# Eight swiglu blocks of a layer as seven-product pairs instead of seven, three plain blocks instead of four, one block instead of three left for the end

## The chip, the cores and the metric

The kernel runs on one core of a Trainium2 chip. The metric is the device time of one execution in microseconds (us); the kernel before was timed three times.

## The reference, cut to what matters

Two layers, each `x += mixer(rmsnorm(x))` and then `x += swiglu(rmsnorm(x))`, on x of 256 frames by 2048 features in float32. The change lies in the second half of both layers:

```
def swiglu(h, w1, w3, w2):
    return (jax.nn.silu(h @ w1) * (h @ w3)) @ w2
```

h is 256 x 2048, w1 and w3 are 2048 x 5632, w2 is 5632 x 2048. The 5632 columns are worked in eleven blocks of 512, numbered 0 to 10.

## The kernel before, in words

**A product.** Every float32 weight tile (128 x 2048, 1 MB) is loaded by a DMA on SP's queue and split into two fp32r parts: ScalarE casts it (`wh`), VectorE subtracts to get the rest (`wl`), both in `split_w` (line 132). Each product then runs three matmuls (high by high, high by low, low by high). A ring of four `raw` tiles holds streamed weights, and rings of three hold `wh` and `wl`.

**Two ways to make a block of w1 and w3.** With the frames cut into two halves and the 2048 inputs into two halves, h @ w1 and h @ w3 of a block are eight half products of 24 matmuls. A plain block does all eight, 192 matmuls and eight splits. `pair` (line 368) does the two weights together with seven products, 168 matmuls, from sums of weights: it splits 14 tiles, forms four sums on VectorE (`plus`, line 405) and four by DMAs on GpSimd's queue that add to what lies in SBUF (`plus_dma`, line 408). Its products run in the order A11, F5, F3, A12, F6, F7, N22. A11 is followed by the sums va + vb, F3 by vb + vc. A DMA adds to va after F5, for F6, and another after F6, for N22. After A12 to N22 come the gates (`done`), which make the block's values. va and vb lie in four tiles of their own (`v0` to `v2`, and `g3`), vc and vd in the raw ring.

**Turning.** A finished block's values are transposed on TensorE and split again (`split_t`, line 208; `turned` in `plain_steps`, line 515), as the left operand of the down product by w2. These steps wait in the queue `side`; `tick`, called after every six or twelve matmuls, runs the next one.

**Order of a layer's swiglu** (`ffn`, line 561). First block 0 by `plain` (line 451), alone. Its first two tiles run before the norm of x is complete (`flush`, then `rstd`). Then seven turns, each a pair with other work between its products: the pair yields after every product, and the work does one step of 24 matmuls in each of eight slots. The work is either a plain block in eight steps (`plain_steps`, line 480) or eight pieces of the down product (`pieces`, line 535), which takes two turned blocks at a time and adds to x:

```
enumerate(((2, 1), (3, None), (4, None), (6, 5), (7, None), (8, None), (10, 9)))
```

The first number is the pair's block, the second the plain block beside it (None: pieces). A pair yields twice after F7, so a turn runs A11, step 0, F5, 1, F3, 2, A12, 3, F6, 4, F7, 5, 6, N22, 7. The three blocks left (8, 9, 10) go to `residual` (line 345), which multiplies them by w2 with nothing beside it. In the first layer this also makes the next norm's operands; in the second it ends with `gemm_tail` (line 140), which does the first 128 frames, then the others, and `last` (line 1125), which scales and stores the result.

The order of instructions on each engine is not quite the program's: at compile time a scheduler lets a later instruction pass an earlier one that it thinks is not ready.

Of the kernel before, what the change touches and what calls it, by code (L numbers as in the profile page):

```python
# [19 lines left out]
P = 128  # L20
# [3 lines left out]
NB = 512  # L24
# [31 lines left out]
def trunk(  # L56
# [55 lines left out]


    side = deque()

    def tick():

# [14 lines left out]
    def split_w(raw, pool=wp):  # L132

        wh = pool.tile([P, 4, NB], F32R, tag="wh", bufs=3 if pool is wp else 1, name="wh")
        wl = pool.tile([P, 4, NB], F32R, tag="wl", bufs=3 if pool is wp else 1, name="wl")
        nc.scalar.copy(wh, raw)  # L136
        nc.vector.tensor_sub(wl, raw, wh.bitcast(F32))  # L137
        return wh, wl

    def gemm_tail(w, c0, parts, pool, done):  # L140
# [228 lines left out]
    def pair(nrm, wa, wb, c0, turn, done):  # L369
# [33 lines left out]
            return nrm.pool.tile([P, NB], F32, tag=tag, bufs=1, name=tag)  # L403

        def plus(dst, other):
            return lambda c: nc.vector.tensor_add(dst[c], dst[c], other[c])  # L406

        def plus_dma(dst, w, j):
            return lambda c: nc.gpsimd.dma_start(dst[c], src(w, j, c), accum_op=ALU.add)
# [30 lines left out]
        product(b3, vb, "F7", False, True)  # L440
        nc.vector.tensor_add(y, y, b3)
        yield
        yield
        product(b3, va, "N22", False, True)
        nc.vector.tensor_sub(s1, s1, b3)
        done("21", s1)
        done("22", y)
        yield

    def plain(nrm, ws, c0, done):  # L450

        for q, w in zip("12", ws):
            acc = [acc_p.tile([P, NB], F32, tag="acc", name="acc") for _ in range(3)]
            for g in range(4):
                raw = wp.tile([P, 4, NB], F32, tag="raw", bufs=RAW, name="raw")
                nc.sync.dma_start(raw, w[g * NB:(g + 1) * NB, c0:c0 + NB].rearrange("(k p) n -> p k n", p=P))
                wh, wl = split_w(raw)
                for bank, form, start, stop in ((0, "A11", True, True), (1, "F7", True, True)) if g < 2 else \
                        ((0, "A12", False, True), (2, "N22", True, True)):
                    hi, lo = nrm.forms[form]  # L460
                    for j in range(4):
                        k = 4 * (g % 2) + j
                        for i, (l_, r_) in enumerate(((hi, wh), (hi, wl), (lo, wh))):
                            nc.tensor.matmul(acc[bank], l_[:, k, :], r_[:, j, :], start=start and k == i == 0,  # L464
                                             stop=stop and k == 7 and i == 2, skip_group_check=not start)
                        if j % 2:
                            tick()
                if g == 1:
                    s1 = nrm.pool.tile([P, NB], F32, tag="s1", bufs=1, name="s1")
                    nc.scalar.copy(s1, acc[0])  # L470
                    nc.vector.tensor_add(s1, s1, acc[1])
                    yield
            nc.vector.tensor_sub(s1, s1, acc[2])
            done("1" + q, acc[0])
            done("2" + q, s1)

    def plain_steps(ws, b, forms, sc, ready):

        flat = res.tile([P, 4 * NB], F32, tag=f"g{b % 3}", name="early")
        us = [flat[:, t * NB:(t + 1) * NB] for t in range(NT)]  # L480
# [51 lines left out]
            yield  # L532

        part = [None, None, b * NB]
        side.append(turned())
        yield part

    def pieces(w, parts):

# [21 lines left out]
    def ffn(layer, nrm):  # L561

        w1, w3, w2 = ffn_w1[layer], ffn_w3[layer], ffn_w2[layer]
        sc = {}
        parts = []
        ready = set()

        def block(b, us):
            def turned():
                yield from split_t(us, hi, lo)  # L570
                ready.add(b * NB)

            hi, lo = hi_lo(b % 3)
            side.append(turned())
            parts.append((hi, lo, b * NB))

        def gate(us):
            def done(q, v):
                t = int(q[0]) - 1
                if q[1] == "1":  # L580
                    us[t] = cm.tile([P, NB], F32, tag="u", name="u")
                    nc.scalar.activation(us[t], v, AF.Silu, scale=sc["r"][:, t:t + 1])
                else:
                    nc.vector.scalar_tensor_tensor(us[t], us[t], sc["r"][:, t:t + 1], v, op0=ALU.mult, op1=ALU.mult)
            return done

        us = [None] * NT
        for slot, _ in enumerate(plain(nrm, (w1, w3), 0, gate(us))):
            if slot == 0:
                flush()  # L590
                sc["r"] = nrm.rstd()
        block(0, us)

        for turn, (b, inner) in enumerate(((2, 1), (3, None), (4, None), (6, 5), (7, None), (8, None), (10, 9))):
            if inner is None:
                two, parts[:2] = parts[:2], []
                work = pieces(w2, two)
            else:
                work = plain_steps((w1, w3), inner, nrm.forms, sc, ready)
            us = [None] * NT  # L600
            made = None
            for slot, _ in enumerate(pair(nrm, w1, w3, b * NB, 1 - turn % 2, gate(us))):
                if inner is None and slot == 0:
                    assert all(r0 in ready for _, _, r0 in two)
                made = next(work)
            if inner is not None:
                parts.append(made)
            block(b, us)
        return w2, parts


# [554 lines left out]
```

## Time and profile before

| | us |
|---|---|
| median of 3 runs | 2260.61 (2259.99 to 2260.88) |
| the profiled execution | 2262.72 |
| its span | 2260.9 |
| TensorE busy | 2226.0 (98%), 10247 matmuls and transposes |
| VectorE busy | 1576.4 (70%) |
| ScalarE busy | 1169.4 (52%) |
| GpSimd busy | 100.1 (4%) |
| DMA | 484.96 MB, 214 GB/s on average |

The span runs from the first to the last instruction; the execution's own time has 1.8 us around it. The mean granted TensorE clock is 0.999 of full speed. A matmul shown as busy for 0.39 us overlaps the next one, so a busy share of 98% does not say by itself that TensorE is at its limit: the distance from the start of one to the start of the next does. In the rows below, PE is TensorE (PEld its weight loads), DVE VectorE, ACT ScalarE, POOL GpSimd, SP the engine that issues most loads.

### The profile page before, as it was taken

What the parts mean: (1) busy time and instruction counts of PE and PEld (TensorE: products, weight loads), DVE (VectorE), ACT (ScalarE), POOL (GpSimd) and SP (SyncE); (2) the same over time, 40 slices, a digit from 0 to 9 for tenths busy, and PEclk for the clock granted to TensorE, in tenths of its full rate; (3) what the DMA queues carried; (4) which work ended last, traced back from release to release, by engine and by line L of the source; (5) the groups of instructions that cost most, each with busy time, mean ns of one, the idle gap of its engine ahead of it and who ended that gap; (6) DMA issues with size and microseconds to landing.
All of it is one profiled execution on the core that took longest, in us unless ns stands there. A gap on an engine that the chain in (4) does not pass through costs nothing.

```text
span 2260.9 us, 25126 instructions
## 1 busy us (share of the span) xinstructions
PE 2226.0 (98%) x10247; PEld 1834.7 (81%) x10247; DVE 1576.4 (70%) x1282; ACT 1169.4 (52%) x1046; POOL 100.1 (4%) x147
## 2 busy tenths in 40 slices
PE   9999999999999999999999999999999999999998
PEld 8888888887787887788888888888888778778787
DVE  6546455778878888876555755556887886887874
ACT  5545455555555555555444544555554555555553
POOL 0000000000000000000100000000000000000000
PEclk9999999999999999999999999999999999999999
DMA  8555465597797797795554555457779779779763
GB/s 289 169 170 188 128 229 184 200 290 223 231 290 219 233 276 228 230 264 179 176 181 150 185 169 168 160 194 242 200 212 313 212 217 310 213 219 304 222 203 111
DMA packets 250547, 484.96 MB, mean 214 GB/s; under 512 B 8072, under 2 KB 20704, under 8 KB 250304
## 3 DMA queue, kind: packets, MB, share of 16 engines
q1 hardware_dynamic: 219856, 423.33, 54.3%
q0 software_dynamic: 29568, 58.72, 15.0%
q8 instruction: 80, 1.31, 0.2%
q10 hardware_dynamic: 1008, 1.31, 0.2%
q14 instruction: 35, 0.29, 0.0%
HBM read 481.20 MB, written 2.12 MB: 214 GB/s over the span
## 4 chain that ended last, share of the span: by engine, by line
PE 81%; DVE 11%; DMA 3%; ACT 2%; issue 2%; SPq 0%; POOL 0%; POOLq 0%; ACTq 0%
PE acc L394 15%; PE acc L202 12%; PE acc L204 12%; PE acc L203 12%; PE half L494 9%; DVE wl L137 4%; PE down L552 4%; PE down L553 4%; PE down L551 4%; DMA raw<-in_ffn_w 3%; PE acc L464 3%; DVE v L406 2%; ACT wh L136 2%; DVE g L406 1%; DVE x L558 1%
## 5 line engine op out<-in xcount | busy, mean ns | idle before, releaser
L136 ACT CAST wh<-raw 128x2048 fp32r<-128x2048 f32 x187 | 358.0, 1915 | 439.4 <-PE down L553 164.3
L137 DVE TENSOR_TENSOR wl<-raw,wh 128x2048 fp32r<-128x2048 f32 x187 | 426.8, 2289 | 204.1 <-ACT wh L136 203.9
L193 DVE TENSOR_TENSOR wl<-raw,wh 128x2048 fp32r<-128x2048 f32 (+3 forms) x161 | 349.9, 2176 | 302.2 <-ACT wh L192 302.1
L192 ACT CAST wh<-raw 128x2048 fp32r<-128x2048 f32 (+3 forms) x161 | 291.9, 1816 | 261.5 <-PE acc L204 211.0
L202 PE MATMUL acc<-wh,hh 128*128 128x512 f32 (+3 forms) x832 | 325.5, 391 | 0.0
L204 PE MATMUL acc<-wh,hl 128*128 128x512 f32 (+3 forms) x832 | 317.3, 381 | 0.0
L203 PE MATMUL acc<-wl,hh 128*128 128x512 f32 (+3 forms) x832 | 316.3, 380 | 0.6 <-DVE wl L193 0.6
L137 DVE TENSOR_TENSOR wl<-v,wh 128x2048 fp32r<-128x2048 f32 x102 | 232.8, 2287 | 24.5 <-ACT wh L136 24.4
L136 ACT CAST wh<-v 128x2048 fp32r<-128x2048 f32 x102 | 195.2, 1913 | 76.6 <-PE acc L394 43.4
L552 PE MATMUL down<-wl,g 128*128 128x512 f32 x512 | 201.3, 393 | 13.7 <-DVE wl L137 13.5
L553 PE MATMUL down<-wh,g 128*128 128x512 f32 x512 | 199.6, 390 | 0.0
L551 PE MATMUL down<-wh,g 128*128 128x512 f32 x512 | 198.3, 391 | 0.0
L203 PEld LDWEIGHTS acc<-wl,hh 128*128 128x128 f32 x832 | 156.7, 188 | 29.5 <-issue 1.7
L204 PEld LDWEIGHTS acc<-wh,hl 128*128 128x128 f32 x832 | 156.3, 188 | 29.5
L202 PEld LDWEIGHTS acc<-wh,hh 128*128 128x128 f32 x832 | 156.5, 188 | 28.6 <-issue 1.9
L394 PE MATMUL acc<-wh,fhF 128*128 128x512 f32 x448 | 174.6, 390 | 0.0
L394 PE MATMUL acc<-wl,fhF 128*128 128x512 f32 x448 | 174.3, 389 | 0.0
L394 PE MATMUL acc<-wh,flF 128*128 128x512 f32 x448 | 174.3, 389 | 0.0
L202 PE MATMUL acc<-wh,g 128*128 128x512 f32 x424 | 167.0, 394 | 0.0
L203 PE MATMUL acc<-wl,g 128*128 128x512 f32 x424 | 165.8, 391 | 0.0
L204 PE MATMUL acc<-wh,g 128*128 128x512 f32 x424 | 165.6, 391 | 0.0
L552 PEld LDWEIGHTS down<-wl,g 128*128 128x128 f32 x512 | 96.1, 188 | 39.2 <-DVE wl L137 20.2
(311 smaller groups left out, 3608.5 us busy)
## 6 DMA issues: line engine op xcount, KB each, us to landing
raw<-in_ffn_w SPq DMA_DIRECT2D x208, 1024.0 KB, 7.0
raw<-in_dsa_w_in SPq DMA_DIRECT2D x48, 1024.0 KB, 5.0
v<-in_ffn_w SPq DMA_DIRECT2D x42, 1024.0 KB, 8.4
raw<-in_gla_w_in SPq DMA_DIRECT2D x40, 1024.0 KB, 5.1
v<-in_ffn_w POOLq DMA_DIRECT2D x40, 1024.0 KB, 9.0
raw<-in_gla_w_out SPq DMA_DIRECT2D x16, 1024.0 KB, 5.0
g<-in_ffn_w POOLq DMA_DIRECT2D x16, 1024.0 KB, 13.0
raw<-in_dsa_w_out SPq DMA_DIRECT2D x16, 1024.0 KB, 4.9
```

The source lines that it names most:

```text
L136: nc.scalar.copy(wh, raw)
L137: nc.vector.tensor_sub(wl, raw, wh.bitcast(F32))
L192: a = nc.scalar.copy(wh[:, sl, :n], raw[:, sl, :n])
L193: v = nc.vector.tensor_sub(wl[:, sl, :n], raw[:, sl, :n], wh[:, sl, :n].bitcast(F32))
L202: nc.tensor.matmul(acc[t][:, :n], hi[:, k, ts_], wh[:, k, :n], start=start, stop=False)
L203: nc.tensor.matmul(acc[t][:, :n], hi[:, k, ts_], wl[:, k, :n], start=False, stop=False)
L204: nc.tensor.matmul(acc[t][:, :n], lo[:, k, ts_], wh[:, k, :n], start=False, stop=last)
L394: nc.tensor.matmul(acc, l_[:, k, :], r_[:, j, :], start=start and k == i == 0, stop=stop and k == 7 and i == 2, skip_group_check=not start)
L494: nc.tensor.matmul(acc[bank], l_[:, k, :], r_[:, j, :], start=start and k == i == 0, stop=stop and k == 7 and i == 2, skip_group_check=not ...
L551: nc.tensor.matmul(acc[t], hi[:, k, ts_], wh[:, k, :], start=start, stop=False)
L552: nc.tensor.matmul(acc[t], hi[:, k, ts_], wl[:, k, :], start=False, stop=False)
L553: nc.tensor.matmul(acc[t], lo[:, k, ts_], wh[:, k, :], start=False, stop=last)
```

## The change

Block 0 is no longer made alone. Its plain steps run beside the pair of block 1: two steps ahead of the pair, then one in six of its eight slots (not in slots 3 and 7). A layer is eight turns: pairs 1, 2, 4, 5, 6, 8, 9, 10; plain blocks 0, 3, 7 beside three of them, pieces beside the other five, so that ten blocks instead of eight are multiplied by w2 beside pairs and one, block 10, is left to `residual`. `plain` goes. The second yield after F7 moves behind N22: N22, step 6, step 7, and the next pair's A11. VectorE's sums are put into a queue, `sums_due`, and `split_w` issues one at the end of each later split, so a sum stands behind the next tile's split. A finished block's turning enters `side` after the next pair's A11 (slot 0), where it entered ahead of it. The DMA loads and the DMA additions of a pair are issued as before.

```diff
     side = deque()
+    sums_due = deque()
...
         nc.scalar.copy(wh, raw)
         nc.vector.tensor_sub(wl, raw, wh.bitcast(F32))
+        if sums_due:
+            sums_due.popleft()()
         return wh, wl
...
         def plus(dst, other):
-            return lambda c: nc.vector.tensor_add(dst[c], dst[c], other[c])
+            return lambda c: sums_due.append(lambda: nc.vector.tensor_add(dst[c], dst[c], other[c]))
...
         product(b3, vb, "F7", False, True)
         nc.vector.tensor_add(y, y, b3)
         yield
-        yield
         product(b3, va, "N22", False, True)
         nc.vector.tensor_sub(s1, s1, b3)
         done("21", s1)
         done("22", y)
         yield
-
-    def plain(nrm, ws, c0, done):
...
+        yield
...
         part = [None, None, b * NB]
-        side.append(turned())
-        yield part
+        yield part, turned()
...
+        late = []
...
             hi, lo = hi_lo(b % 3)
-            side.append(turned())
+            late.append(turned())
             parts.append((hi, lo, b * NB))
...
-        us = [None] * NT
-        for slot, _ in enumerate(plain(nrm, (w1, w3), 0, gate(us))):
-            if slot == 0:
-                flush()
-                sc["r"] = nrm.rstd()
-        block(0, us)
-
-        for turn, (b, inner) in enumerate(((2, 1), (3, None), (4, None), (6, 5), (7, None), (8, None), (10, 9))):
+        for turn, (b, inner) in enumerate(((1, 0), (2, None), (4, 3), (5, None), (6, None), (8, 7), (9, None), (10, None))):
...
+            if turn == 0:
+                next(work)
+                next(work)
+                flush()
+                sc["r"] = nrm.rstd()
             us = [None] * NT
             made = None
             for slot, _ in enumerate(pair(nrm, w1, w3, b * NB, 1 - turn % 2, gate(us))):
-                if inner is None and slot == 0:
-                    assert all(r0 in ready for _, _, r0 in two)
-                made = next(work)
+                if slot == 0:
+                    side.extend(late)
+                    late.clear()
+                if inner is None and slot < 2:
+                    assert two[slot][2] in ready
+                if turn or slot not in (3, 7):
+                    made = next(work)
+                if turn == 0 and slot == 6:
+                    side.append(made[1])
             if inner is not None:
-                parts.append(made)
+                parts.append(made[0])
+                if turn:
+                    late.append(made[1])
             block(b, us)
+        side.extend(late)
         return w2, parts
```

## Rows read from the trace of the kernel before

**Rows 1.** The page, part 1: busy time of each engine.
```profile
PE 2226.0 (98%) x10247; PEld 1834.7 (81%) x10247; DVE 1576.4 (70%) x1282; ACT 1169.4 (52%) x1046; POOL 100.1 (4%) x147
```

**Rows 2.** Windows: length; busy PE, PEld, DVE, ACT, POOL; clock, DMA share, GB/s.
```profile
394.08:438.94 44.86, 44.77 (x201) 36.75 (x200) 30.51 (x26) 24.36 (x26) 0.70 (x1) 1.00 0.70 234
438.94:1034.08 595.14, 584.90 (x2593) 478.48 (x2592) 478.72 (x298) 322.92 (x205) 36.53 (x28) 1.00 0.83 242
...
1589.89:2185.55 595.66, 584.75 (x2593) 478.59 (x2592) 478.94 (x298) 322.91 (x205) 36.36 (x28) 1.00 0.83 241
```

**Rows 3.** Timeline of PE (start, us): first matmul of F3, of step 2.
```profile
547.58 0.39 PE L394 MATMUL acc<-wh,fhF 128*128 128x512 f32 x1
...
553.02 0.39 PE L551 MATMUL down<-wh,g 128*128 128x512 f32 x1
```

**Rows 4.** Waits of PE over the whole run: us in total, times, longest.
```profile
PE down L552 <- DVE wl L137: 13.5, 12, 1.6
PE half L494 <- DVE wl L137: 7.3, 6, 1.6
```

**Rows 5.** Timeline of PE: the first piece after A11 (a scheduled F5 matmul within).
```profile
614.34 0.61 PE L551 MATMUL down<-wh,g 128*128 128x512 f32 x2
614.80 0.39 PE L394 MATMUL acc<-wh,fhF 128*128 128x512 f32 x1
616.77 0.50 PE L552 MATMUL down<-wl,g 128*128 128x512 f32 x1 [1.58 <-DVE wl L137]
```

**Rows 6.** Timeline of DVE ahead of that wait.
```profile
608.82 2.28 DVE L137 TENSOR_TENSOR wl<-g,wh 128x2048 fp32r<-128x2048 f32 x1
...
611.62 2.28 DVE L406 TENSOR_TENSOR g<-g,v 128x2048 f32<-128x2048 f32 x1
613.83 0.69 DVE L219 TENSOR_TENSOR g<-tr,g 128x512 fp32r<-128x512 f32 x1
614.43 2.28 DVE L137 TENSOR_TENSOR wl<-raw,wh 128x2048 fp32r<-128x2048 f32 x1
```

**Rows 7.** Timeline of PE: first matmuls of F6 and N22 of the first turn.
```profile
484.17 0.39 PE L394 MATMUL acc<-wh,fhF 128*128 128x512 f32 x1
...
511.37 0.39 PE L394 MATMUL acc<-wh,fhN 128*128 128x512 f32 x1
```

**Rows 8.** Timeline of POOL: the second addition to va of that turn.
```profile
490.75 1.30 POOL L409 DMA_DIRECT2D g<-in_ffn_w  x1 [8.13 <-issue]
```

**Rows 9.** Line 409, time to landing: that addition alone, then all 56.
```profile
DMA to landing us min/median/max: 13.7/13.7/13.7
...
DMA to landing us min/median/max: 8.5/9.7/15.6
```

**Rows 10.** Timeline of DVE, ACT and PE before a wait at step 3.
```profile
803.86 2.29 DVE L406 TENSOR_TENSOR v<-v,raw 128x2048 f32<-128x2048 f32 x1
...
816.13 1.91 ACT L136 CAST wh<-raw 128x2048 fp32r<-128x2048 f32 x1 [3.52 <-DMA raw<-in_ffn_w]
...
820.42 0.50 PE L552 MATMUL down<-wl,g 128*128 128x512 f32 x1 [0.66 <-DVE wl L137]
```

**Rows 11.** Timeline of SP: last load of a pair's vb behind the norm.
```profile
405.34 0.50 SPq L381 DMA_DIRECT2D v<-in_ffn_w  x1
```

**Rows 12.** DMA issues: that kind of load, KB each, median us to landing.
```profile
v<-in_ffn_w SPq DMA_DIRECT2D x42, 1024.0 KB, 8.4
```

**Rows 13.** Timeline of all engines where the first layer's last block is turned.
```profile
1039.22 0.66 PE L216 MATMUL tr<-ident,u 128*128 128x128 f32 x4
...
1040.53 1.36 DVE L219 TENSOR_TENSOR g<-tr,g 128x512 fp32r<-128x512 f32 x2 [0.77 <-ACT g L218]
```

**Rows 14.** Timeline of DVE in `residual` of the first layer.
```profile
1056.81 0.87 DVE L257 SCALAR_TENSOR_TENSOR hl<-tr,cols,hh 128x256 fp32r<-128x256 f32 x2
```

**Rows 15.** Timeline of DVE at the end: the first 128 frames' last operations.
```profile
2244.89 0.69 DVE L1127 TENSOR_TENSOR x<-x,acc 128x512 f32<-128x512 f32 x1 [5.85 <-PE acc L155]
...
2247.86 0.74 DVE L1134 SCALAR_TENSOR_TENSOR x<-x,rf,nf 128x512 f32<-128x512 f32 x1
```

More of the change, by code (lines that the diff above doesn't have):

```diff
@@ L448, in pair @@
         yield
-    def plain(nrm, ws, c0, done):
[L452 to L475, printed above, removed]
+        yield
     def plain_steps(ws, b, forms, sc, ready):
```

## The prediction

> **What bounds the kernel now.** I read the page's engine shares first, then the length of the turns by windows, then the distance between matmul starts, and last the waits. TensorE is busy for 98% of the span, VectorE for 70%, ScalarE for 52% [rows 1]. The windows show that a layer's seven turns take 595.14 and 595.66 us and block 0 alone 44.86, with VectorE busy for 478.72 of the 595.14, 80% [rows 2]. A busy matmul proves little, so the starts decide: from F3's first matmul to that of the next step, 24 matmuls later, pass 5.44 us, 0.2267 each [rows 3]. A pair with its step work is 168 + 192 = 360 matmuls, 81.6 us of a turn's mean 85.0 (595.14 / 7). So TensorE's stream is the bound, and 3.4 us a turn are transposes or waits.
>
> The waits are all for VectorE's `wl`: 13.5 us in 12 waits beside pieces, 7.3 in 6 beside plain steps [rows 4]. Each costs more than its listed idle time, since the last matmul before it overlaps: where 1.58 us are listed, the starts lie 1.97 apart instead of 0.23, so 1.74 are lost, 0.16 more [rows 5]. The 18 waits cost 20.8 + 18 x 0.16 = 23.7 us.
>
> Why VectorE is late is seen ahead of that wait. It works without a gap: the split of A11's second tile, a sum, the second of two subtractions that turn the last block, and only then, from 614.43 to 616.71, the split that the piece waits for [rows 6]. The piece's first matmul had started at 614.34 [rows 5].
>
> **The change part by part.**
>
> *Matmuls.* Block 0 goes from 192 to 168; the down product is moved, not changed. That is 24 fewer a layer, 48 x 0.2267 = **-10.9 us**, wholly on TensorE's stream. The number of transposes stays. The Trainium skill, TensorE: Matmul & The Clock Gate, section "Wait — 56ns, not 53.3ns?", gives 215.7 ns for a warm matmul of 512 columns; by that the 48 would be worth 10.4 us, and this trace's 0.2267 decides.
>
> *What the eighth pair adds.* Six more splits, four sums and four DMA additions a layer, less the plain block's few adds. VectorE has 595.14 - 478.72 = 116 us free in seven turns, ScalarE more [rows 2], so as totals they hide behind matmuls, at nothing. Without that cover six splits and four sums of 2.28 [rows 6] would be 23 us a layer. Only their places matter, which follow.
>
> *The first step after A11.* The second sum (2.28) and two subtractions of the turning (0.69 each) come behind the piece's split instead of ahead of it, so the split would end at 616.71 - 3.66 = 613.05, before the step's start at 614.34 [rows 5, 6]. Late next is F5: its two splits are needed at 614.34 + 5.44 = 619.78 and 2.72 later. VectorE does the second sum, to 615.3, F5's first split, to 617.6, two turning subtractions, to 619.0, and the second split, to 621.3: before 622.5, with 1.2 to spare. Two more subtractions after a plain block use that up. I take no wait here; the bounds are 0 and today's 1.74.
>
> *Step 3.* Its raw tile can be loaded only after the sum vb + vc has read the tile that it replaces. That sum ended at 806.15, ScalarE then idled for the load until 816.13, and TensorE for 0.66 [rows 10]. The sum is queued one split later now, up to 2.28. But VectorE has less ahead of it, and the scheduler may draw it forward. I take 0.4 us a turn, from 0 to 0.66 + 2.28, nearer to today's row.
>
> *N22, one step earlier.* Step 6 moves behind N22, so N22 starts four groups after F6 instead of five: 21.8 us instead of 27.2 [rows 3, 7]. Its second tile needs the second DMA addition, which GpSimd issued at 490.75 and which landed 13.7 later, at 504.45, 20.3 after F6's start [rows 7 to 9]. A cast of 1.91 [rows 10] and a split of 2.28 make 24.5; N22's second half needs it at 21.8 + 2.7 + 0.2 = 24.7. That just fits: a landing after 20.5 is a wait. The slowest of the 56 additions took 15.6 [rows 9], 1.9 more, a wait of 1.7. I take 0.3 a turn, from 0 to 1.7. Behind N22's splits on SP's queue stand the loads of the next vb, which gain a step.
>
> *Turns 1 and 0.* Without work in slot 7 of turn 0, N22 is followed by A11 at once: four splits and a sum, 11.4 us of VectorE, and three small operations of 0.7, in 10.9 us of matmuls. I take 1.5 us of wait in turn 1, from 0 to twice 1.74. In turn 0 the pair's loads of vb stand on SP behind the norm: the last was issued at 405.34 [rows 11] and lands about 8.4 later [rows 12], 413.7. A sum, a cast and a split make 420.2. F5's second half wants it after two plain steps, A11 and one step: from 394.08 four groups, 21.8, block 0's own 1.3 of transposes and wait (44.86 - 192 x 0.2267), and 2.9 make 420.1 [rows 2]. VectorE need not be free at once, so 0.6, from 0 to a whole load's 8.4 if SP's order is worse.
>
> *Waits after.* Twelve later turns at 0.7 are 8.4, turns 0 and 1 of both layers 1.2 + 3.0: 12.6 against 23.7 now, **-11.1 us**.
>
> *The end of a layer.* Block 10's turned values are needed at once, where blocks 8 and 9 covered them. From the transposes' start at 1039.22 the first subtraction ends at 1041.2, the second at 1041.9, 2.0 and 2.7 us later [rows 13]. Eight transposes fill about 1.0 of it, and two products that want the high part alone 0.45. I take 1.0 a layer, from 0.3 to 2.7: **+2.0**. The eight pieces that leave `residual` carry 192 matmuls, eight loads and eight adds to x, which the turns take in as they do today's. `residual` keeps 24 matmuls a group, 5.4 us; a split of 2.28, two adds of 0.69 [rows 15] and four norm subtractions of 0.44 [rows 14] fill 5.4 on VectorE. It only just fits: **+1.0** for both layers, from 0 to 4. At the very end the first 128 frames' chain on VectorE runs from 2244.89 to 2248.60, 3.7 us [rows 15]; the others' twelve matmuls cover 2.7 of it: **+1.0**, from 0 to 3.7.
>
> Sum: -10.9 - 11.1 + 2.0 + 1.0 + 1.0 = -18.0. The profiled execution took 2262.7 us around its span of 2260.9; it goes to 2244.7. It lies 2.1 above the median of the runs, so the median goes to **2242.6 us**.
>
> **Rivals.**
>
> *The turn keeps its length.* The scheduler draws the sums forward again, or VectorE sets the pace. Then eight turns of 85.0 us stand against 44.86 + 595.14: +40.0 a layer, less the 192 matmuls that leave `residual`, 43.5: -3.5. Both layers -7.0, ends +4.0: 2257.6, no change. For it: VectorE is 80% busy [rows 2], and the scheduler already moves matmuls past waiting ones [rows 5]. Against it: 3.7 us of VectorE work are written behind the place of the wait. The Trainium skill, Perfetto Trace Analysis, section "Identifying the Most-Contended Engine", speaks for it: it judges TensorE by LDWEIGHTS' busy share, here 478.48 of 595.14, 80%, so that a fifth would be free and fewer matmuls would give little; the even 0.2267 from start to start speaks against that [rows 3].
>
> *The waits move to the loads.* The first step's wait goes, but step 3 and N22 wait 1.5 us a turn. Sixteen turns cost 24, so the waits give nothing: -10.9 + 4.0, 2253.7. For it: DMA engines 83% busy in the turns [rows 2] and N22's fit of 0.2 us.
>
> *Slower: N22 waits for the DMA additions.* The place is N22's second half, 16 times. If each of the two additions before it takes 2 us longer, because the loads beside them are packed closer, the second lands 24.3 after F6, a wait of 3.8, and 16 x (3.8 - 0.3) = 56: 2299. It decides from a mean wait of 18.0 / 16 + 0.3 = 1.4 us, a landing 21.9 after F6, 1.6 later than in rows 7 to 9. At 15.6 everywhere it would be 2242.6 + 16 x 1.4 = 2265. Against it: the slowest of 56 is that 15.6. The Trainium skill, DMA: Bandwidth & Descriptors, section "Queues, rings and completion order", says that a DMA engine takes turns between queues, packet by packet; by that rule more loads on SP's queue take no larger share from GpSimd's, and the price ends near 2265. No run here shows it.
>
> **How the numbers follow.** A measurement of this kernel can tell about 0.2%, 4.5 us. The forecast (2231 to 2250) has a chance of 0.70, the waits moved to the loads 0.13, a turn of the same length 0.08, slower 0.05, and 0.04 is for nearly no wait at all, below 2231. All below 2256.1 is faster by over 0.2%: 0.70 + 0.13 + 0.04 = 0.87; within it 0.08; slower 0.05. The range reaches down to waits of 0.1 a turn and half the cost at the ends (-10.9 - 22.1 + 2.0, about 2230) and up past the waits moved to the loads, 2255.
>
> **What would show it.** Right: PE's waits in the turns fall to half or less, the 1.6 us wait at the first step is gone, a turn takes 82 to 84 us, and the first product of block 10 in `residual` starts 1 to 2 us after its transposes. Wrong: TensorE stopped at N22 while ScalarE waits for line 409's landing; waits at step 3 behind a load of over 10 us; a sum still ahead of the first step's split; a stop of several us between the first plain steps and F5 of turn 0.

## The result, and the profile after

The changed kernel took 2238.52 us, the median of four runs (2233.39 to 2240.16), against 2260.46 for the kernel before beside it: a ratio of 0.9899, 95% interval 0.9882 to 0.9916, 21.9 us less. The forecast was 2242.6, with a range of 2230 to 2255. The profiled execution took 2237.55, 25.2 less than that of before; the ledger below is made on these two.

The page of the changed kernel, part 1, which answers to [rows 1]:

```profile
span 2235.8 us, 25156 instructions
PE 2209.4 (99%) x10199; PEld 1829.1 (82%) x10199; DVE 1630.7 (73%) x1320; ACT 1192.8 (53%) x1056; POOL 110.4 (5%) x155
```

TensorE has 48 matmuls fewer, VectorE 54 us more work. The waits of PE in the changed kernel, which answer to [rows 4]:

```profile
PE acc L397 <- DVE wl L138: 4.6, 3, 1.8
PE acc L205 <- ACT g L221: 3.2, 2, 1.6
PE acc L397 <- ACT wh L137: 2.2, 2, 1.3
PE acc L207 <- DVE g L222: 0.8, 2, 0.5
PE down L529 <- DVE wl L138: 0.2, 1, 0.2
```

The 18 waits at pieces and plain steps, 20.8 us, are gone but for 0.2. New ones stand in a pair's own products (L397, five waits) and in `residual` (L205, L207). Where they lie is seen in windows of the changed kernel: all turns of the first layer with the two steps ahead of them, its turns 0 to 3, and all turns of the second layer. The columns are as in [rows 2].

```profile
394.15:1063.79 669.64, 666.20 (x2969) 549.73 (x2968) 557.48 (x353) 375.35 (x246) 43.08 (x37) 1.00 0.85 249
405.98:481.97 75.99, 72.87 (x314) 59.55 (x312) 60.63 (x36) 43.04 (x27) 5.41 (x4) 0.98 0.88 260
481.97:566.49 84.52, 84.20 (x377) 68.87 (x376) 73.31 (x48) 45.83 (x29) 5.17 (x4) 1.00 0.85 249
566.49:649.10 82.61, 82.61 (x370) 68.40 (x369) 67.84 (x42) 47.25 (x31) 5.19 (x4) 1.00 0.87 255
649.10:732.60 83.50, 83.50 (x377) 69.03 (x376) 70.95 (x46) 45.96 (x29) 5.19 (x4) 1.00 0.84 252
...
1532.63:2201.28 668.65, 664.82 (x2969) 548.58 (x2968) 557.19 (x353) 377.40 (x247) 42.23 (x33) 1.00 0.85 250
```

From turn 2 on TensorE is busy all of a turn, 82.6 to 83.5 us against a mean of 85.0 before; in turn 0 it is idle for 3.12 us and in turn 1 for 0.32, which is all of the 3.44 in the first layer's turns.

**The ledger.** What a layer's turns take over their matmuls at 0.2267 us: before, 44.86 + 595.14 - 2712 x 0.2267 = 25.2 in the first layer and 25.7 in the second [rows 2]; after, 669.64 - 2880 x 0.2267 = 16.7, and 15.8. That is 18.4 less. Behind the turns the same count gives 1.4 more in the first layer and 2.6 in the second, 4.0. With 48 x 0.2267 = 10.9 for the matmuls: -10.9 - 18.4 + 4.0 = -25.3, and the spans differ by 25.1. One more thing moved with the work: eight transposes a layer (block 9's), which stood behind the turns, now stand in them. They start 0.109 us apart, so 0.9 us a layer went from the ends into the turns; without that the turns fell by some 20.1 and the ends rose by some 5.8.

**The two new stops.** The first is N22 of turn 0. The timeline of PE in the changed kernel:

```profile
469.98 0.49 PE L397 MATMUL acc<-wh,fhN 128*128 128x512 f32 x1 [1.29 <-ACT wh L137]
472.31 0.58 PE L397 MATMUL acc<-wl,fhN 128*128 128x512 f32 x1 [1.83 <-DVE wl L138]
472.69 0.63 PE L397 MATMUL acc<-wh,flN 128*128 128x512 f32 x1
...
475.68 0.55 PE L397 MATMUL acc<-wh,fhN 128*128 128x512 f32 x1
```

ScalarE, whose cast N22 waits for, waits in its turn for the second DMA addition. The timelines of ScalarE and of GpSimd there:

```profile
468.03 1.90 ACT L137 CAST wh<-g 128x2048 fp32r<-128x2048 f32 x1 [8.26 <-DMA g<-in_ffn_w]
...
443.41 1.29 POOL L413 DMA_DIRECT2D v<-in_ffn_w  x1 [16.70 <-DVE wl L138]
453.59 1.30 POOL L413 DMA_DIRECT2D g<-in_ffn_w  x1 [8.89 <-issue]
```

The second addition was issued only when the first had landed, at 453.3, and took 14.3 us itself, to 467.9. That is 23.9 after F6's start at 444.1; the prediction had put the limit at 20.5. By the starts, the two waits cost 1.45 and 2.10 us. Behind them the matmuls start 0.427 us apart for 3 us.

The second stop is at the end of a layer. The timelines of PE and of ScalarE where block 10 is turned in the first layer, which answer to [rows 13]:

```profile
1063.80 1.03 PE L219 MATMUL tr<-ident,u 128*128 128x128 f32 x8
1066.43 0.50 PE L205 MATMUL acc<-wh,g 128*128 128x512 f32 x1 [1.60 <-ACT g L221]
...
1063.99 1.90 ACT L195 CAST wh<-raw 128x2048 fp32r<-128x2048 f32 x1 [3.48 <-PE down L530]
1065.80 1.06 ACT L221 CAST g<-tr 128x512 fp32r<-128x512 f32 x2
```

The transposes are done in 1.03 us, but ScalarE has begun a cast of weights and copies the turned values after it. The first product starts 2.63 us after the transposes' start and 1.60 after their end. By the starts this costs 1.77 us, and the wait for VectorE's part of the same values (L207) 0.48 more; in the second layer the two are 1.77 and 0.68.

### The profile page after: what moved, and what is told of

The parts are those of the page before. It is cut to its first block, busy times and chain, and to the rows that moved or that the text cites. A ratio compares the mean times of both kernels' runs of the same rounds, so it can differ in the third digit from the quotient of the medians.

```text
span 2235.8 us, 25156 instructions
## 1 busy us (share of the span) xinstructions
PE 2209.4 (99%) x10199; PEld 1829.1 (82%) x10199; DVE 1630.7 (73%) x1320; ACT 1192.8 (53%) x1056; POOL 110.4 (5%) x155
## 4 chain that ended last, share of the span: by engine, by line
PE 80%; issue 12%; DMA 3%; DVE 3%; ACT 1%; POOL 1%; POOLq 0%; SPq 0%; ACTq 0%; DVEq 0%
PE acc L397 19%; PE acc L207 11%; PE acc L205 11%; PE acc L206 11%; PE half L472 10%; PE down L529 4%; PE down L530 4%; PE down L528 4%; DMA g<-in_ffn_w 2%; DVE wl L138 1%; DMA v<-in_ffn_w 1%; POOL v L413 1%; ACT wh L137 1%; PE tr L219 1%; PE trq L883 0%
## 5 line engine op out<-in xcount | busy, mean ns | idle before, releaser
L138 DVE TENSOR_TENSOR wl<-raw,wh 128x2048 fp32r<-128x2048 f32 x193 | 440.4, 2289 | 139.6 <-ACT wh L137 139.5
L196 DVE TENSOR_TENSOR wl<-raw,wh 128x2048 fp32r<-128x2048 f32 (+3 forms) x147 | 317.7, 2164 | 274.5 <-ACT wh L195 274.4
L195 ACT CAST wh<-raw 128x2048 fp32r<-128x2048 f32 (+3 forms) x147 | 265.2, 1807 | 229.8 <-PE acc L207 193.7
L205 PE MATMUL acc<-wh,hh 128*128 128x512 f32 (+3 forms) x832 | 325.5, 391 | 0.0
L207 PE MATMUL acc<-wh,hl 128*128 128x512 f32 (+3 forms) x832 | 317.4, 381 | 0.0
L138 DVE TENSOR_TENSOR wl<-v,wh 128x2048 fp32r<-128x2048 f32 x120 | 274.0, 2288 | 42.2 <-ACT wh L137 42.2
L137 ACT CAST wh<-v 128x2048 fp32r<-128x2048 f32 x120 | 229.7, 1914 | 114.0 <-PE acc L397 64.3
L529 PE MATMUL down<-wl,g 128*128 128x512 f32 x640 | 249.5, 390 | 0.5 <-DVE wl L138 0.2
L528 PE MATMUL down<-wh,g 128*128 128x512 f32 x640 | 250.0, 391 | 0.0
L530 PE MATMUL down<-wh,g 128*128 128x512 f32 x640 | 249.3, 390 | 0.0
L397 PE MATMUL acc<-wh,fhF 128*128 128x512 f32 x512 | 200.1, 391 | 0.0
L397 PE MATMUL acc<-wh,flF 128*128 128x512 f32 x512 | 199.7, 390 | 0.0
L397 PE MATMUL acc<-wl,fhF 128*128 128x512 f32 x512 | 199.6, 390 | 0.0
L207 PEld LDWEIGHTS acc<-wh,hl 128*128 128x128 f32 x832 | 156.3, 188 | 29.4
L205 PEld LDWEIGHTS acc<-wh,hh 128*128 128x128 f32 x832 | 156.5, 188 | 28.6 <-issue 1.9
L530 PEld LDWEIGHTS down<-wh,g 128*128 128x128 f32 x640 | 120.1, 188 | 25.2
L528 PEld LDWEIGHTS down<-wh,g 128*128 128x128 f32 x640 | 120.1, 188 | 24.6
L205 PE MATMUL acc<-wh,g 128*128 128x512 f32 x312 | 123.4, 396 | 3.2 <-ACT g L221 3.2
```

What stands on the lines that cost most here:

```text
L195: a = nc.scalar.copy(wh[:, sl, :n], raw[:, sl, :n])
L196: v = nc.vector.tensor_sub(wl[:, sl, :n], raw[:, sl, :n], wh[:, sl, :n].bitcast(F32))
L205: nc.tensor.matmul(acc[t][:, :n], hi[:, k, ts_], wh[:, k, :n], start=start, stop=False)
L207: nc.tensor.matmul(acc[t][:, :n], lo[:, k, ts_], wh[:, k, :n], start=False, stop=last)
L397: nc.tensor.matmul(acc, l_[:, k, :], r_[:, j, :], start=start and k == i == 0, stop=stop and k == 7 and i == 2, skip_group_check=not start)
L528: nc.tensor.matmul(acc[t], hi[:, k, ts_], wh[:, k, :], start=start, stop=False)
```

## The experiments

The kernel before ran beside each group: 2260.99, 2260.56 and 2260.98 us, medians of nine runs each. Lines of code are those of the changed kernel unless said otherwise.

### The deferrals undone, one by one and together

```diff
-            return lambda c: sums_due.append(lambda: nc.vector.tensor_add(dst[c], dst[c], other[c]))
+            return lambda c: nc.vector.tensor_add(dst[c], dst[c], other[c])
```

> The changed kernel, with VectorE's four sums of a pair issued at once again, ahead of the next tile's split; turning, N22's place and the eighth pair stay as changed. Theory A (VectorE's order ahead of the first step was the wait, and the sum is the larger part of it): the step's split ends 2.28 us later than it could, about 1 us after it is needed, so a wait of about 1 us comes back at the first step of some 14 turns, and the kernel takes 8 to 15 us more than the changed one (about 2247 to 2253). Rival B (the turning behind A11, or N22's earlier place, is what freed VectorE): not over 3 us more than the changed one, about 2239 to 2241.

2246.72 us (2246.15 to 2249.64), 8.2 above the changed kernel, at the low edge of what the deferral's theory asked for. The waits of PE in it:

```profile
PE down L529 <- DVE wl L138: 3.5, 6, 1.3
...
PE half L472 <- DVE wl L138: 2.9, 3, 1.3
```

The waits at the steps are back, but for 6.4 us, not for 20.8. Something else in the change must have emptied the rest.

```diff
-            late.append(turned())
+            side.append(turned())
...
-                    late.append(made[1])
+                    side.append(made[1])
```

> The changed kernel, with a finished block's turning put into the queue at once, ahead of the next A11, as before the change; the sums stay late. Theory A: two subtractions of 0.69 us lie ahead of the first step's split again, and that split has 1.3 us to spare, so 0 to 4 us more than the changed kernel (2238 to 2243). Rival B (the turning is what freed VectorE): the 1.7 us waits come back, 14 turns, 15 to 24 us more (2253 to 2262).

2241.95 us (2240.73 to 2244.47), 3.4 above the changed kernel, as the first theory had it. Then both together:

> The changed kernel with both deferrals undone: eight turns per layer, N22 earlier, but VectorE's sums issued at once and the values turned ahead of the next A11. Theory A (the parts add up): 8.2 + 3.4 above the changed kernel, about 2250, 2248 to 2252. Rival B (the deferrals take the same waits, and without either the 1.58 us at the first step of a turn and the waits of the down steps are back): 16 to 21 above it, 2254 to 2260, so that eight turns alone gain next to nothing.

2248.87 us (2247.09 to 2250.35), 11.0 above the 2237.86 of the changed kernel beside it. The parts add up, and the rival, for which the waits of before had to come back whole, falls. Its waits of PE at steps:

```profile
PE down L529 <- DVE wl L138: 3.9, 6, 1.4
...
PE half L472 <- DVE wl L138: 3.6, 3, 1.6
```

With nothing deferred, 7.5 us of the 20.8 are there. So the eighth turn or N22's place had removed 13 us of them.

### The deferrals alone, seven turns

The kernel before, with `sums_due` as in the change's diff and with its seven turns' turning deferred:

```diff
-            side.append(turned())
+            late.append(turned())
...
+                if slot == 0:
+                    side.extend(late)
+                    late.clear()
                 made = next(work)
             if inner is not None:
-                parts.append(made)
+                parts.append(made[0])
+                late.append(made[1])
             block(b, us)
+        side.extend(late)
```

> The kernel before with the two deferrals alone: VectorE's sums behind the next split, and the turning of the values behind the next A11. Seven turns per layer, the plain block in front of them and N22's place stay. Theory A (the deferrals and the eighth turn add up: undone one by one in the changed kernel they cost 8.2 and 3.4 us): 11 to 13 less than the kernel before, 2247 to 2250. Rival B (the two deferrals take the same waits, the 20.8 us of rows 4, and only both together empty them; what the eighth turn gains in matmuls it pays in turn 0): 16 to 21 less, 2239 to 2245.

2234.37 us (2234.06 to 2234.88), 26.2 below the kernel before: below both theories, and 3.5 below the changed kernel beside it. Its turns by windows, first layer and second:

```profile
394.04:1019.86 625.82, 625.73 (x2793) 516.03 (x2792) 508.97 (x323) 348.54 (x231) 37.22 (x29) 1.00 0.82 247
1530.81:2156.51 625.70, 625.61 (x2794) 516.13 (x2793) 508.86 (x323) 348.56 (x231) 37.05 (x29) 1.00 0.83 247
```

TensorE is idle for 0.09 us in 625.82, and a layer's turns take 11.0 us over their matmuls, transposes for the most part, where they took 25.2. The deferrals without the eighth turn empty the waits whole; in the changed kernel, with eight turns and N22 earlier, they are worth 11. This also is about the floor of the count: with seven turns, what a layer has above 11.0 is stops. With eight turns the floor lies near 11.9, since eight more transposes stand in them.

### N22's place alone, and the eighth turn alone

In the kernel before:

```diff
         nc.vector.tensor_add(y, y, b3)
         yield
-        yield
         product(b3, va, "N22", False, True)
...
         done("22", y)
         yield
+        yield
```

> The kernel before with N22 a step earlier, directly behind step 5, and the empty step at the end of the turn; nothing deferred, seven turns. Theory A (N22's last results then leave VectorE's queue a whole step before the next A11, so this alone empties a good part of the waits of rows 4, the same that the deferrals empty): 8 to 15 less than the kernel before, 2246 to 2253. Rival B (as the prediction had it, 0.3 us per turn and no more): at most 5 less, 2255.5 to 2260.

2236.89 us (2236.81 to 2238.66), 24.1 below the kernel before: more than the theory asked for, and far from the prediction's view. The windows of its turns, its wait of PE at plain steps (at pieces none is listed), and VectorE's timeline ahead of the first step after A11 of turn 2, to be held against [rows 6]:

```profile
394.36:1021.34 626.98, 626.37 (x2793) 516.09 (x2792) 511.12 (x323) 347.83 (x231) 37.22 (x29) 1.00 0.82 247
```

```profile
PE half L494 <- DVE wl L137: 0.2, 1, 0.2
```

```profile
596.53 0.68 DVE L444 TENSOR_TENSOR s<-s,acc 128x512 f32<-128x512 f32 x1
...
599.32 0.75 DVE L584 SCALAR_TENSOR_TENSOR u<-u,rstd,y 128x512 f32<-128x512 f32 x1
...
604.51 2.28 DVE L137 TENSOR_TENSOR wl<-g,wh 128x2048 fp32r<-128x2048 f32 x1
...
607.91 2.29 DVE L406 TENSOR_TENSOR g<-g,v 128x2048 f32<-128x2048 f32 x1
...
610.72 2.28 DVE L137 TENSOR_TENSOR wl<-raw,wh 128x2048 fp32r<-128x2048 f32 x1
```

The operations are those of [rows 6] (A11's split, the sum, the turning, the step's split), but the second subtraction of the turning now comes behind the step's split, at 612.91. And N22's results (L444, L584) are worked off at 596.5 to 600.1, a whole step ahead of A11, which starts at 605.77. Before, they came at 604.2 to 607.7, between A11's own splits. So all that follows is early: the step's split ends at 613.00 instead of 616.71, for a step that starts 2.2 us earlier (612.15 against 614.34), so that 0.3 us are lost there by the starts instead of 1.75. The same backlog of VectorE is emptied in two ways, by moving N22's results ahead of it or by moving sums and turning behind the split, and with seven turns either alone does nearly all of it.

The changed kernel with both deferrals undone, as above, and N22 back in its place:

```diff
         nc.vector.tensor_add(y, y, b3)
         yield
+        yield
         product(b3, va, "N22", False, True)
...
         yield
-        yield
```

> The changed kernel with both deferrals undone and N22 back behind two steps: of the change the eighth turn alone is left. Theory A (the 20.8 us of waits of rows 4 are then back, 16 steady turns for 12, and the end of the layer costs 2 per layer): the 10.9 us of matmuls less, 4 for the ends and 0 to 8 for the further turns and turn 0 more, 2250 to 2261. Rival B (N22's place carries none of it): as the run with both deferrals undone, 2247 to 2250, or less by the 3.6 us that N22's place gave before, 2244 to 2247.

2271.19 us (2269.13 to 2274.97), a ratio of 1.0048 (1.0035 to 1.0060): slower than before by 10.2, the only one of these, and above both theories. Its turns by windows (first layer), and its waits of PE:

```profile
394.03:1078.75 684.72, 670.51 (x2969) 548.56 (x2968) 556.60 (x353) 374.73 (x246) 42.54 (x35) 1.00 0.82 244
```

```profile
PE down L529 <- DVE wl L138: 18.7, 12, 2.8
PE half L472 <- DVE wl L138: 9.1, 6, 1.6
```

There are 27.8 us of waits at the steps against 20.8, the longest 2.8 in turn 1, where N22 and A11 follow each other without a step. The excess of the first layer is 31.8 us against 25.2. Set side by side, with the excess of the turns over their matmuls (us, first and second layer):

| turns | N22 | deferred | median, us | excess |
|---|---|---|---|---|
| 7 | late | no (before) | 2260.5 | 25.2, 25.7 |
| 7 | earlier | no | 2236.9 | 12.2, 12.7 |
| 7 | late | yes | 2234.4 | 11.0, 10.9 |
| 8 | late | no | 2271.2 | 31.8, 33.0 |
| 8 | earlier | no | 2248.9 | 20.5, 21.7 |
| 8 | late | yes | 2234.9 | 14.1, 13.8 |
| 8 | earlier | yes (changed) | 2238.5 | 16.7, 15.8 |

In the three settings that were run with seven and with eight turns, the kernel with eight takes 10.2 (against the kernel before beside it), 12.0 and 0.5 us more. The 10.9 us of matmuls that the eighth turn saves show in none of them. (Seven turns with both N22 earlier and the deferrals weren't run.)

### Turn 0's N22

```diff
         product(b3, vb, "F7", False, True)
         nc.vector.tensor_add(y, y, b3)
         yield
+        yield
         product(b3, va, "N22", False, True)
...
-        yield
```

> The changed kernel, with N22 one step later, as before the change (F7, step 5, step 6, N22, step 7). Theory A (the wait at N22 of turn 0, 3.5 us in the first layer with the slower clock behind it and 3.2 in the second, is for the second DMA addition, which lands 23.9 and 23.5 us after F6 while 20.5 is needed): N22 comes 5.4 us later, the wait goes, 6 to 9 us fewer there; the later turns lose 0 to 0.5 each, so the kernel takes 8 us less to 1 us more than the changed one (2230 to 2240). Rival C (N22's earlier place is what removed the waits of the steady turns): 10 to 20 us more (2248 to 2258).

2234.89 us (2232.48 to 2236.51), 3.6 below the changed kernel, though the runs of the two overlap. The rival's 10 to 20 us more did not come: with the deferrals there, the later turns don't need N22's earlier place, and in turn 0 it costs a stop. That stop is gone; 0.7 us of waits for L138 remain in L397, and two waits in turn 1:

```profile
PE down L529 <- DVE wl L138: 2.1, 2, 1.2
```

The other way to give the addition time is to keep step 3, so that A12 and F6 are not back to back in turn 0:

```diff
-                if turn or slot not in (3, 7):
+                if turn or slot not in (2, 7):
```

> The changed kernel, with turn 0's two empty slots at 2 and 7 instead of 3 and 7, so that a plain step again lies between A12 and F6. Theory A (without step 3 the ring of three split tiles lets F6's first split be made only when A12 begins, so the first addition is issued 0.6 us ahead of F6 instead of 2.9, and the second lands too late): the first is issued about 2.9 ahead of F6 again, the second lands 20 to 21.5 after it, the wait at N22 falls from 3.5 and 3.2 us to under 1.2 in both layers, and with it the stretch of slower clock; 5 to 9 us less than the changed kernel (2230 to 2234). Rival D (the additions land late because the loads at the start of a layer are packed closely): landing stays at 23 or more and the time within 2 us of the changed kernel.

2235.85 us (2232.97 to 2237.43), 2.7 below, less than the first theory asked for, and the stop is still there in the trace: N22 in the first layer waits at 470.26 and 472.59. The timeline of GpSimd in turn 0 and, below, the windows of the first addition and of its counterpart in turn 2:

```profile
441.97 1.29 POOL L413 DMA_DIRECT2D v<-in_ffn_w  x1 [14.93 <-DVE wl L138]
454.31 1.30 POOL L413 DMA_DIRECT2D g<-in_ffn_w  x1 [11.05 <-issue]
```

```profile
442.00:454.00 12.00, 12.00 (x55) 9.93 (x54) 8.70 (x5) 6.33 (x4) 1.25 (x1) 1.00 1.09 320
...
607.80:616.30 8.50, 8.50 (x40) 7.02 (x38) 5.60 (x4) 5.14 (x4) 1.29 (x1) 1.00 0.96 209
```

The first addition was now issued 2.9 us ahead of F6, as in the later turns, but took 12.0 us where it takes 8.5 there: the DMA engines moved 320 GB/s beside it against 209. The second landed 23.4 and 23.1 us after F6, where the rival asked for 23 or more (the time moved by 0.7 more than it allowed). So with the step back the stop stays, and the loads packed there are what is left; that they cause it is argued from these rows, not shown. Taking such a load away, or running the two additions side by side, wasn't tried, and what gave the 2.7 us (the runs lie 4.5 apart) stays open.

### The end of the layer, and both stops together

```diff
+                if slot == 7 and turn == 7:
+                    block(b, us)
+                    side.extend(late)
+                    late.clear()
                 if turn or slot not in (3, 7):
...
-            block(b, us)
+            if turn < 7:
+                block(b, us)
```

> The turning of block 10 goes into the last inner step of turn 7, so that it lies in front of the residual's first weights on every queue. Theory A (the stop of 2.63 us at 1063.80 and the like one of the second layer is a ScalarE cast of weights queued ahead of the turned block's copy): about 2.0 to 2.3 us less per layer, 4 less than the changed kernel beside it, allowing 2 to 5. Rival B (the stop is the wait for the block's last result, which VectorE makes, and moves into step 7 with the turning): within 1 of the changed kernel beside it, with a wait of TensorE in front of the transposes in place of the one behind them.

2229.80 us (2228.84 to 2230.47), 8.1 below the changed kernel beside it, more than expected. The timeline of PE in place of the stop of 2.63 us:

```profile
1062.01 0.60 PE L219 MATMUL tr<-ident,u 128*128 128x128 f32 x4
1062.37 0.48 PE L205 MATMUL acc<-wh,g 128*128 128x512 f32 x1
```

The first product starts 0.36 us after the first of the last four transposes, since the block's other values were turned inside step 7. Behind the turns the count gives 2.75 and 2.96 us less than in the changed kernel, 5.7 in all; some 1.8 of the rest lies in the turns, where N22's stop of turn 0 was shorter in this execution (waits of 0.52 and 2.10 us in the first layer).

This is also where the eighth turn begins to pay: 2229.80 is 4.6 below the 2234.37 of seven turns with the deferrals, run beside it, and no run of one reaches a run of the other.

Then the last block turned early and N22 later:

```diff
         nc.vector.tensor_add(y, y, b3)
         yield
+        yield
         product(b3, va, "N22", False, True)
...
-        yield
...
+                if slot == 7 and turn == 7:
+                    block(b, us)
+                    side.extend(late)
+                    late.clear()
```

> The changed kernel with N22 back behind two inner steps (as in the second group) and block 10 turned in the last inner step. Theory A (the stop at turn 0's N22 and the stop at the end of the layer are separate, and what they cost adds up): below either alone, 2225 to 2229. The floor by the kernel before with the deferrals alone is 2234.4 less 48 matmuls of 0.2267 us, 2223.5. Rival B (what N22's wait cost is paid at the first steps of turn 1 instead, 1.0 to 1.4 us there in either layer): within 1.5 of the 2229.8 of the early turning alone.

2230.72 us (2230.00 to 2231.57): no better than the early turning alone, as the rival had it. The stop at N22 is gone, but turn 1 waits (0.80 and 0.94 us by the starts), in the second layer turn 0's transposes wait for VectorE (0.96), and at that layer's end a wait of 1.1 us for the turned values stays. Turn 1's wait isn't at the first step, where the rival looked for it, but at step 3, behind A12. The timelines of ScalarE and of PE there:

```profile
514.28 1.91 ACT L137 CAST wh<-raw 128x2048 fp32r<-128x2048 f32 x1 [5.50 <-DMA raw<-in_ffn_w]
...
518.58 0.50 PE L529 MATMUL down<-wl,g 128*128 128x512 f32 x1 [0.64 <-DVE wl L138]
```

ScalarE stood idle for 5.50 us for step 3's tile. Its load was issued at 505.70, right behind the end of a split on VectorE at 505.67, and took 8.5 us. So it is a chain like that of the prediction's step 3: a late VectorE frees a tile late, and the load comes late. The two waits in turn 1 of the kernel with only N22 later (2.1 us together) stand at the same place.

And that kernel with turn 0's empty steps moved:

```diff
-                if turn or slot not in (3, 7):
+                if turn or slot not in (2, 7):
```

> The run of this group with N22 later and block 10 turned early, and turn 0's empty steps at 2 and 7 in place of 3 and 7. Theory A (the waits of 1.0 to 1.4 us in turn 1 come from VectorE's backlog out of turn 0, which one more step between A12 and F6 thins out): 1 to 3 less than that run. Rival B (they come from the missing step between N22 and the next A11, which stays missing): within 1 of it.

2231.16 us (2230.46 to 2234.60), the rival's "within 1". Turn 1's wait is still there (1.96 and 1.16 us by the starts, in the profile of the slowest of the four runs), again at step 3, in the first layer behind a load of 9.7 us issued at 506.83. So putting back the step between A12 and F6 doesn't remove it. Whether the missing step between N22 and the next A11 is what makes VectorE free that tile late is not shown.

Last, the changed kernel unaltered, a second time:

> The changed kernel once more, beside the runs of this group. If its spread of 6.8 us comes from the stop at turn 0's N22 (the last term of seven) and a clock that sometimes falls behind it, the median lies at 2236 to 2240 again and the runs some 5 to 7 us apart; if the spread was of the first group of runs alone, they lie within 2 us of each other.

2237.86 us (2237.18 to 2239.88). The median came again; the spread of 2.7 us lies between the two theories. That the N22 stop makes it isn't borne out: the early turning alone keeps that stop and has runs 1.6 apart, the late N22 has lost it and has runs 4.0 apart. The spread stays open.

The fastest kernel here is the changed one with its last block turned in step 7, 2229.80, a ratio of 0.9863 (0.9849 to 0.9876) to the kernel before.

## Why the prediction was right, and where its terms were not

**The result** lies in the range and on the side forecast, 4.1 us below the predicted time. On the profiled executions the forecast was -18.0 and the change -25.2. That it came so near is in part luck: the misses below go both ways.

**Matmuls, -10.9.** 48 fewer, at the distance of [rows 3]: as predicted as a count. What the sum doesn't show is that here the eighth turn costs all of it. Compared with seven turns and the deferrals (2234.4), the changed kernel's turns have 5.7 and 4.9 us more of excess and its ends 3.6, 14.2 in all.

**Waits after, 12.6 instead of 23.7.** This is the term that was mis-sized, in both directions. The step "Twelve later turns at 0.7 are 8.4" failed: from turn 2 on TensorE hardly stops (0.3 us by the starts, both layers together), and neither step 3 (0.4 taken, 0 to 2.94 kept) nor N22 (0.3 taken) waits there. Turns 0 and 1, on the other hand, lost 8.5 us and 1.7 more at a lower clock, where 4.2 had been taken. Together that is 10.5, near the 12.6, by two errors that nearly cancel. The turns gained some 6 us more in distances between starts that were lengthened by less than 0.25 us each, which the sum of 23.7 did not hold. The ranges of both terms reached down to 0, but step 3's was read near a wait of the kernel before [rows 10], and that wait stood behind a VectorE in arrears: it is gone also where N22 alone was moved.

**N22, one step earlier, +0.3 a turn.** This was booked as a cost alone, a question of whether the DMA addition lands in time. Its other side, what N22's results do on VectorE's queue, was not followed, and in the kernel before it is worth 24.1 us alone. The forecast of the mechanism (VectorE's queue ahead of the first step) was right, but it took one of two sufficient remedies for the only one.

**The first step after A11.** "I take no wait here" was right: 0.2 us are listed in the whole run. Undoing the deferral of the sums costs 8.2 and that of the turning 3.4.

**Turn 0 and turn 1.** For turn 0 the prediction took 0.6 us at F5's second half, behind a late load; no wait is there. Instead N22 stops for 1.45 + 2.10 us in the first layer and 1.06 + 2.10 in the second. The prediction named this place under "wrong" (N22 while ScalarE waits for an addition) and had the limit, 20.5 after F6, about right. What failed is the landing, 20.3 after F6, which it took from a turn of the kernel before and did not work out for turn 0, where it was 23.9 and 23.5. The step that is missing there between A12 and F6 does not explain it, since the stop stays with the step put back. Turn 1 has 0.65 and 1.11, inside the 1.5 taken, but not where it was looked for: not at A11 behind VectorE, but mostly at A12 and step 3, where a tile's load came late.

**The ends, +4.0.** Measured 4.0, 1.4 in the first layer and 2.6 in the second, where 1.5 and 2.5 had been taken. The agreement is luck: 1.7 of transposes had left the ends for the turns, which the sum did not hold, so the stops there cost some 5.8. Of the parts only the turning can be told apart. Its first product started 1.60 us after the transposes' end, inside the 1 to 2 forecast, but with the second wait it cost 2.25 and 2.45 us where 1.0 a layer was taken, since ScalarE's cast of the next weights stood ahead of the copy. The Trainium skill, PSUM — Partial Sum Buffer, section "Engine vs sequencer instructions", says that ScalarE's and VectorE's queues are strictly first in, first out; the rows at 1063.99 and 1065.80 agree.

**The rivals.** A turn of the same length: with the deferrals and N22's place both left out, eight turns stayed near 85 us and the kernel was slower, so this rival's mechanism was real for the kernel without them. Its witness, the share of LDWEIGHTS, did not decide: with the deferrals alone PEld is busy for 516.03 of 625.82 us, 82%, and TensorE is idle for 0.09. The Trainium skill, Perfetto Trace Analysis, section "Identifying the Most-Contended Engine", judges TensorE's headroom by LDWEIGHTS' busy share beside the rate of useful work (MFU); read by that share alone, nearly a fifth would be free, and this trace does not agree. The waits moved to the loads in turns 0 and 1 alone. The slower rival, N22 waiting in all 16 turns, needed landings 21.9 after F6; that came in turn 0 only, where it was 23.9 and 23.5 (20.0 at most in the other turns). All 64 additions of the changed kernel (min, median, max to landing), against [rows 9]:

```profile
DMA to landing us min/median/max: 8.5/9.7/14.3
```

## What to carry to other kernels

A wait at one place of an in-order engine's queue can often be emptied by moving any one of the things ahead of it: try each part of a change alone, for here N22's place (-24) and the deferrals (-26) each did nearly the whole, and the third part, fewer matmuls, gave nothing on top of either until the last block was turned a step earlier (4.6 us below the best kernel of seven turns). When a step is moved, follow what it issues on every queue at both ends, what arrives earlier as well as what may now be late. And at the seams (first turn, last block) count which steps are missing: the steady turns ran without a stop, and nearly all that the change left on the table lay in turn 0, turn 1 and the two ends.

## What the runs showed of the hardware

Behind the stop at N22 in turn 0, TensorE ran at a lower granted clock (PEclk, the third number from the end). Windows of the changed kernel in the first layer; below them the same of the kernel with the last block turned early, and its window behind the stop of the second layer:

```profile
469.90:472.50 2.60, 0.69 (x2) 0.38 (x3) 2.54 (x2) 2.60 (x3) 0.00 (x0) 1.00 0.53 206
472.50:476.30 3.80, 3.80 (x11) 2.93 (x11) 3.80 (x2) 1.03 (x1) 0.00 (x0) 0.55 0.73 231
```

```profile
469.90:472.50 2.60, 1.19 (x5) 1.01 (x6) 2.60 (x2) 2.60 (x2) 0.00 (x0) 1.00 0.49 172
472.50:476.30 3.80, 3.80 (x19) 3.13 (x18) 3.80 (x4) 1.96 (x3) 0.00 (x0) 1.00 1.01 358
...
1606.60:1610.10 3.50, 3.50 (x11) 2.68 (x10) 3.48 (x3) 0.36 (x2) 0.00 (x0) 0.52 0.99 331
```

A mean of 0.55 of full speed over 3.8 us is close to the lower of the two levels, 1.2 of 2.4 GHz, and the matmuls start 0.427 us apart there instead of 0.2267. From 472.31 to 476.06 the changed kernel starts nine matmuls in 3.75 us, where 9 x 0.2267 = 2.04 would do: 1.7 us lost on top of the stop. The second kernel has the stop too, a little shorter, and keeps the full clock in the first layer, but not in the second (0.52). In the changed kernel it is the other way about: in its second layer a like stop has no such stretch behind it; in its repeat both layers have one. So a stop's price here is its length and sometimes half as much again; what decides is not shown.
